# Row variances: other rows per partition, 64 KiB per partition and load, a quarter of each row on ScalarE

## Chip, cores, metric

One core of a Trainium2 chip. The metric is the device time of one execution in microseconds (us); lower is better. A profile's span is about 1.8 us shorter than the measured time of the same execution. A packet is one record of a DMA engine's work, here one contiguous piece, one partition's share of a load. A load has landed, or is ready, when the last of the sixteen DMA engines has reported its share.

## The reference

```python
x: float32 (8192, 8192)
return np.var(x, axis=1)          # 8192 float32
```

The input is 268.4 MB. It has to be read once, and nothing else of any size is moved.

## The kernel before

A tile is 128 adjacent rows, one per partition, 32 KiB each. It is loaded by two DMAs of half a row, one on SyncE's queue and one on ScalarE's, into one of four buffers. VectorE does all sums: sixteen `bn_stats` (count, mean and sum of squares of a group of 512 elements) and one `bn_aggr` (which combines the groups) per row.

```python
FMAX = nc.vector.BN_STATS_FMAX                     # 512
x_t = x.rearrange("(t p) (s f) -> t p s f", p=P, f=FMAX)
out_t = out.rearrange("(t p) -> t p", p=P)
data = ctx.enter_context(tc.tile_pool(name="data", bufs=4))
...
def issue_dma(t):
    xt = data.tile([P, nsub, FMAX], mybir.dt.float32)
    for c in range(CH):                            # CH = 2
        dma_eng[c % 2].dma_start(out=xt[:, lo:hi, :], in_=x_t[t, :, lo:hi, :])

def compute(t):
    for j in range(nsub):                          # nsub = 16
        nc.vector.bn_stats(out=st[:, j, :], in_=xt[:, j, :])
    nc.vector.bn_aggr(out=mv, in_=st)
    nc.gpsimd.tensor_copy(out=var_all[:, t : t + 1], in_=mv[:, 1:2])
... # load tile t, compute tile t - 3
nc.tensor.transpose(vp, var_all, ident)            # [128, 64] -> [64, 128]
nc.scalar.copy(vs, vp)
nc.sync.dma_start(out=out_t, in_=vs)
```

Of the kernel before, what the change touches and what calls it, by code (L numbers as in the profile page):

```python
# [1 line left out]

# [5 lines left out]


@with_exitstack  # L10
def kernel(
    ctx: ExitStack,
    tc: tile.TileContext,
    x: bass.AP,
    out: bass.AP,
):
    nc = tc.nc
    P = 128
    n, m = x.shape

    FMAX = nc.vector.BN_STATS_FMAX
    assert m % FMAX == 0
    nsub = m // FMAX

    assert n % P == 0
    ntiles = n // P

    x_t = x.rearrange("(t p) (s f) -> t p s f", p=P, f=FMAX)
    out_t = out.rearrange("(t p) -> t p", p=P)

    data = ctx.enter_context(tc.tile_pool(name="data", bufs=4))
    stats = ctx.enter_context(tc.tile_pool(name="stats", bufs=8))
    singles = ctx.enter_context(tc.tile_pool(name="singles", bufs=1))
    psum = ctx.enter_context(tc.tile_pool(name="psum", bufs=1, space=bass.MemoryType.PSUM))
    outp = ctx.enter_context(tc.tile_pool(name="outp", bufs=1))

    var_all = singles.tile([P, ntiles], mybir.dt.float32)
    ident = singles.tile([P, P], mybir.dt.float32)
    make_identity(nc, ident)

    dma_eng = [nc.sync, nc.scalar]

    CH = 2
    spc = nsub // CH

    xts = [None] * ntiles
    LOOK = 3

    def issue_dma(t):
        xt = data.tile([P, nsub, FMAX], mybir.dt.float32)  # L50
        for c in range(CH):
            lo = c * spc
            hi = lo + spc
            dma_eng[c % 2].dma_start(out=xt[:, lo:hi, :], in_=x_t[t, :, lo:hi, :])  # L54
        xts[t] = xt

    def compute(t):
        xt = xts[t]
        st = stats.tile([P, nsub, nc.vector.BN_STATS_DIM], mybir.dt.float32)
        for j in range(nsub):  # L60
            nc.vector.bn_stats(out=st[:, j, :], in_=xt[:, j, :])  # L61
        mv = stats.tile([P, nc.vector.BN_AGGR_DIM], mybir.dt.float32)
        nc.vector.bn_aggr(out=mv, in_=st)  # L63
        nc.gpsimd.tensor_copy(out=var_all[:, t : t + 1], in_=mv[:, 1:2])  # L64

    for t in range(ntiles):
        issue_dma(t)
        if t >= LOOK:
            compute(t - LOOK)
    for t in range(ntiles - LOOK, ntiles):  # L70
        compute(t)

    vp = psum.tile([ntiles, P], mybir.dt.float32)
    nc.tensor.transpose(vp, var_all, ident)  # L74
    vs = outp.tile([ntiles, P], mybir.dt.float32)
    nc.scalar.copy(vs, vp)  # L76
    nc.sync.dma_start(out=out_t, in_=vs)


# [1 line left out]
_INS = ['x']  # L81
_OUTS = [((8192,), 'float32')]


# [23 lines left out]
```

## Time and profile before

655.47 us, median of 2 runs (655.24 to 655.69).

| | before |
|---|---|
| VectorE busy | 636.2 of 653.6 us |
| VectorE, one tile | 9.93 us |
| DMA, one tile (4.19 MB at 428 GB/s) | 9.80 us |
| last tile landed, first fifteen engines / sixteenth | 630.7 / 638.5 us |

Lines of the page of the kernel before: span; busy time, share and instruction count of each engine; busy tenths and GB/s in 40 equal slices; the chain that ended last by engine; the costliest group (busy us, mean ns of one, idle time before and what ended it).

```profile
span 653.6 us, 1512 instructions
...
PE 0.4 (0%) x1; PEld 0.1 (0%) x1; DVE 636.2 (97%) x1088; ACT 1.5 (0%) x2; POOL 12.4 (2%) x70
...
DVE  2999999999999999999999999999999999999997
...
DMA  8999999999999999999999999999999999999950
GB/s 369 433 430 425 427 432 428 425 431 428 427 428 430 427 427 430 427 427 428 428 426 431 427 429 427 426 429 428 428 427 430 427 428 429 429 425 430 429 222 2
...
DVE 88%; DMA 6%; issue 5%; SPq 0%; PE 0%; ACT 0%; POOLq 0%; POOL 0%
...
L61 DVE BATCH_NORM_STATS2 st<-xt 128x6 f32<-128x512 f32 x1024 | 610.1, 673 | 13.6 <-DMA xt<-in_x_dram 13.6
```

VectorE is busy 97% of the span and leads the chain with 88%; its `bn_stats` waited only 13.6 us for data, nearly all of it for the first tile. The DMA is full too, in all but the last two slices. The windows of the same kernel (length, busy us and instruction count of each engine, granted clock, DMA share, GB/s):

```profile
core 0: us, PE busy (x) PEld busy (x) DVE busy (x) ACT busy (x) POOL busy (x), PEclk, DMA share, GB/s
0.00:20.00 20.00, 0.00 (x0) 0.00 (x0) 7.14 (x13) 0.00 (x0) 0.70 (x6) 1.00 0.91 380
20.00:40.00 20.00, 0.00 (x0) 0.00 (x0) 19.79 (x35) 0.00 (x0) 0.37 (x2) 1.00 1.01 431
...
100.00:600.00 500.00, 0.00 (x0) 0.00 (x0) 500.00 (x856) 0.00 (x0) 9.16 (x50) 1.00 1.01 428
```

Here is the margin: the DMA moves 428 GB/s at a busy share of 1.0, which is 9.80 us per tile; VectorE uses 422 GB/s, 9.93 us per tile. VectorE is the bound by 1.3%. The end, in the chain in order of time (start, length, what):

```profile
630.40 8.91 DVE st L61 x16
...
639.77 0.58 DVE mv L63
...
650.18 0.43 PE vp L74
```

VectorE starts the last tile at 640.3 us, and the last share of that tile had landed at 638.5.

### The profile page before, as it was taken

How to read it: one execution, taken by the hardware profiler on the slowest of the kernel's cores; microseconds unless marked ns; L12 is line 12 of the kernel's file. 1: busy time of each engine (PE TensorE's matmuls, PEld its weight loads, DVE VectorE, ACT ScalarE, POOL GpSimd, SP SyncE). 2: the span in 40 equal slices, each digit the busy share in tenths (PEclk: the TensorE clock that was granted, in tenths of full speed). 3: DMA queues.
4: the chain of work that ended last, by engine and by line, in shares of the span. 5: the costliest groups of instructions: out<-in, count | busy, mean ns of one | idle time of the engine just before them, and what ended most of it. 6: DMA issues, size and time to landing. Idle time of an engine off the chain costs nothing.

```text
span 653.6 us, 1512 instructions
## 1 busy us (share of the span) xinstructions
PE 0.4 (0%) x1; PEld 0.1 (0%) x1; DVE 636.2 (97%) x1088; ACT 1.5 (0%) x2; POOL 12.4 (2%) x70
## 2 busy tenths in 40 slices
PE   0000000000000000000000000000000000000000
PEld 0000000000000000000000000000000000000000
DVE  2999999999999999999999999999999999999997
ACT  0000000000000000000000000000000000000000
POOL 0000000000000000000000000000000000000000
DMA  8999999999999999999999999999999999999950
GB/s 369 433 430 425 427 432 428 425 431 428 427 428 430 427 427 430 427 427 428 428 426 431 427 429 427 426 429 428 428 427 430 427 428 429 429 425 430 429 222 2
DMA packets 18524, 268.57 MB, mean 411 GB/s; under 512 B 2064, under 2 KB 2128, under 8 KB 2128
## 3 DMA queue, kind: packets, MB, share of 16 engines
q1 hardware_dynamic: 9296, 134.25, 48.4%
q10 hardware_dynamic: 9216, 134.22, 48.2%
q14 instruction: 12, 0.10, 0.0%
HBM read 268.44 MB, written 0.03 MB: 411 GB/s over the span
## 4 chain that ended last, share of the span: by engine, by line
DVE 88%; DMA 6%; issue 5%; SPq 0%; PE 0%; ACT 0%; POOLq 0%; POOL 0%
DVE st L61 82%; DMA xt<-in_x_dram 6%; DVE mv L63 5%; SPq L54 0%; PE vp L74 0%; ACT vs L76 0%; POOLq L103 0%; POOL var_all L64 0%
## 5 line engine op out<-in xcount | busy, mean ns | idle before, releaser
L61 DVE BATCH_NORM_STATS2 st<-xt 128x6 f32<-128x512 f32 x1024 | 610.1, 673 | 13.6 <-DMA xt<-in_x_dram 13.6
L63 DVE BATCH_NORM_AGGREGATE mv<-st 128x2 f32<-128x96 f32 x64 | 36.4, 570 | 0.1
L64 POOL COPY var_all<-mv 128x1 f32<-128x1 f32 x64 | 11.7, 183 | 637.1 <-DVE mv L63 637.1
L76 ACT ACT_TABLE_LOAD x1 | 1.3, 1283 | 609.9 <-DMA xt<-in_x_dram 609.9
L74 PE MATMUL vp<-ident,var_all 128*64 128x128 f32 x1 | 0.4, 421 | 650.2 <-POOL var_all L64 650.2
L76 ACT COPY vs<-vp 64x128 f32<-64x128 f32 x1 | 0.3, 258 | 39.5 <-PE vp L74 39.5
masks.py:199 POOL TENSOR_SCALAR_AFFINE_SELECT ident<-ident 128x128 f32<-128x128 f32 x1 | 0.3, 292 | 0.1
L74 PEld LDWEIGHTS vp<-ident,var_all 128*64 128x64 f32 x1 | 0.1, 128 | 650.2 <-POOL var_all L64 650.2
masks.py:197 POOL MEMSET ident<- 128x128 f32 x1 | 0.2, 204 | 0.3 <-POOLq L92 0.3
L92 POOL MEMSET const-float32-0.0<- 128x1 f32 x1 | 0.1, 98 | 0.2 <-issue 0.2
L92 POOL MEMSET const-bfloat16-1.0<- 128x1 bf16 x1 | 0.1, 101 | 0.0
L92 POOL MEMSET const-uint8-127<- 128x1 uint8 x1 | 0.1, 101 | 0.0
L92 POOL MEMSET const-float32-1.0<- 128x1 f32 x1 | 0.1, 98 | 0.0
## 6 DMA issues: line engine op xcount, KB each, us to landing
xt<-in_x_dram ACTq DMA_DIRECT2D x64, 2048.0 KB, 29.1
xt<-in_x_dram SPq DMA_DIRECT2D x64, 2048.0 KB, 28.9
out_dram<-vs SPq DMA_DIRECT2D x1, 32.0 KB, 1.8
```

Of the source, the lines that this page charges most:

```text
L61: nc.vector.bn_stats(out=st[:, j, :], in_=xt[:, j, :])
L63: nc.vector.bn_aggr(out=mv, in_=st)
L64: nc.gpsimd.tensor_copy(out=var_all[:, t : t + 1], in_=mv[:, 1:2])
L74: nc.tensor.transpose(vp, var_all, ident)
L76: nc.scalar.copy(vs, vp)
L92: nc = _bacc.Bacc("TRN2", target_bir_lowering=False, num_devices=1)
```

## The change

Its intent: take a quarter of the sums from VectorE, use long contiguous reads, drop the transposition of the output. Each partition owns 64 adjacent rows. One load is two rows of each partition (64 KiB contiguous, 8 MiB in all), on one queue, into one of three buffers. ScalarE sums the last quarter of each row in two passes (sum and sum of squares about the mean of the first group), GpSimd turns that into the form that `bn_aggr` takes. The last row comes in shrinking pieces, so that little is left to do when the last one lands.

```diff
-    x_t = x.rearrange("(t p) (s f) -> t p s f", p=P, f=FMAX)
-    out_t = out.rearrange("(t p) -> t p", p=P)
-    data = ctx.enter_context(tc.tile_pool(name="data", bufs=4))
+    x_t = x.rearrange("(p t j) f -> t p (j f)", p=P, j=J)          # J = 2
+    out_p = out.rearrange("(p r) -> p r", p=P)
+    data = ctx.enter_context(tc.tile_pool(name="data", bufs=3))
...
+    def row_stats(xt, j):
+        for c in range(DC):                                        # 12 groups of 512
+            bn(st, c, xt[:, o + c * F : o + (c + 1) * F])
+        k = st[:, 1:2]
+        src = xt[:, o + DC * F : o + m]                            # 2048 elements
+        nc.scalar.activation(out=junk, in_=src, func=ACTF.Identity, bias=k, scale=-1.0,
+                             accum_out=s12[:, 0:1])
+        nc.scalar.activation(out=junk, in_=src, func=ACTF.Square, bias=k, scale=-1.0,
+                             accum_out=s12[:, 1:2])
+        ... # five small GpSimd operations put (count, mean, sum of squares) into st
...
+    for t in range(NT - 1):                                        # NT = 32
+        xt = data.tile([P, J * m], FP32, name="xt")
+        nc.sync.dma_start(out=xt, in_=x_t[t])
+        ... # row_stats of both rows, bn_aggr one row later
+    nc.sync.dma_start(out=xt[:, 0:m], in_=x_t[t, :, 0:m])          # last load: row 62
+    pieces = [4096, 2048, 1024, 512, 256, 256]                     # row 63, all on VectorE
...
-    nc.tensor.transpose(vp, var_all, ident)
-    nc.scalar.copy(vs, vp)
-    nc.sync.dma_start(out=out_t, in_=vs)
+    nc.sync.dma_start(out=out_p, in_=var_all[:].rearrange("p t j -> p (t j)"))
```

The 128 pieces of one load used to start 32 KiB apart in HBM. Now they start 64 rows apart, which is 2 MiB.

More of the change, by code (lines that the diff above doesn't have):

```diff
@@ L5 @@
 from concourse import bass_utils, mybir
-from concourse.masks import make_identity
 from concourse._compat import with_exitstack
+FP32 = mybir.dt.float32
+ACTF = mybir.ActivationFunctionType
+ALU = mybir.AluOpType
 @with_exitstack
@@ L19 @@
     n, m = x.shape
-    FMAX = nc.vector.BN_STATS_FMAX
-    assert m % FMAX == 0
-    nsub = m // FMAX
-    assert n % P == 0
-    ntiles = n // P
-    x_t = x.rearrange("(t p) (s f) -> t p s f", p=P, f=FMAX)
-    out_t = out.rearrange("(t p) -> t p", p=P)
-    data = ctx.enter_context(tc.tile_pool(name="data", bufs=4))
-    stats = ctx.enter_context(tc.tile_pool(name="stats", bufs=8))
+    F = nc.vector.BN_STATS_FMAX
+    J = 2
+    NT = n // (P * J)
+    C = m // F
+    AC = 4
+    DC = C - AC
@@ L33 @@
+    NA = AC * F
+    T3 = 3
+    x_t = x.rearrange("(p t j) f -> t p (j f)", p=P, j=J)
+    out_p = out.rearrange("(p r) -> p r", p=P)
+    data = ctx.enter_context(tc.tile_pool(name="data", bufs=3))
+    stats = ctx.enter_context(tc.tile_pool(name="stats", bufs=6))
+    small = ctx.enter_context(tc.tile_pool(name="small", bufs=6))
     singles = ctx.enter_context(tc.tile_pool(name="singles", bufs=1))
     psum = ctx.enter_context(tc.tile_pool(name="psum", bufs=1, space=bass.MemoryType.PSUM))
-    outp = ctx.enter_context(tc.tile_pool(name="outp", bufs=1))
@@ L37 @@
-    var_all = singles.tile([P, ntiles], mybir.dt.float32)
-    ident = singles.tile([P, P], mybir.dt.float32)
-    make_identity(nc, ident)
-    dma_eng = [nc.sync, nc.scalar]
-    CH = 2
-    spc = nsub // CH
-    xts = [None] * ntiles
-    LOOK = 3
-    def issue_dma(t):
-        xt = data.tile([P, nsub, FMAX], mybir.dt.float32)
-        for c in range(CH):
-            lo = c * spc
-            hi = lo + spc
-            dma_eng[c % 2].dma_start(out=xt[:, lo:hi, :], in_=x_t[t, :, lo:hi, :])
-        xts[t] = xt
@@ L57, in compute @@
-    def compute(t):
-        xt = xts[t]
-        st = stats.tile([P, nsub, nc.vector.BN_STATS_DIM], mybir.dt.float32)
-        for j in range(nsub):
-            nc.vector.bn_stats(out=st[:, j, :], in_=xt[:, j, :])
-        mv = stats.tile([P, nc.vector.BN_AGGR_DIM], mybir.dt.float32)
-        nc.vector.bn_aggr(out=mv, in_=st)
-        nc.gpsimd.tensor_copy(out=var_all[:, t : t + 1], in_=mv[:, 1:2])
-    for t in range(ntiles):
-        issue_dma(t)
-        if t >= LOOK:
-            compute(t - LOOK)
@@ L70, with bn @@
-    for t in range(ntiles - LOOK, ntiles):
-        compute(t)
-    vp = psum.tile([ntiles, P], mybir.dt.float32)
-    nc.tensor.transpose(vp, var_all, ident)
-    vs = outp.tile([ntiles, P], mybir.dt.float32)
-    nc.scalar.copy(vs, vp)
-    nc.sync.dma_start(out=out_t, in_=vs)
+    var_all = singles.tile([P, NT, J], FP32)
+    junk = psum.tile([P, NA], FP32)
+    def bn(st, at, src):
+        nc.vector.bn_stats(out=st[:, at * 6 : at * 6 + 6], in_=src)
+    def row_stats(xt, j):
+        st = stats.tile([P, DC * 6 + T3], FP32)
+        s12 = small.tile([P, 2], FP32)
+        tmp = small.tile([P, 2], FP32)
+        o = j * m
+        for c in range(DC):
[6 more added lines that the diff above has]
+                             accum_out=s12[:, 1:2])
+        b = DC * 6
+        nc.gpsimd.memset(st[:, b : b + 1], float(NA))
+        nc.gpsimd.tensor_scalar(out=tmp[:, 0:1], in0=s12[:, 0:1], scalar1=1.0 / NA, scalar2=0.0,
+                                op0=ALU.mult, op1=ALU.add)
+        nc.gpsimd.tensor_tensor(out=st[:, b + 1 : b + 2], in0=k, in1=tmp[:, 0:1], op=ALU.subtract)
+        nc.gpsimd.tensor_tensor(out=tmp[:, 1:2], in0=s12[:, 0:1], in1=tmp[:, 0:1], op=ALU.mult)
+        nc.gpsimd.tensor_tensor(out=st[:, b + 2 : b + 3], in0=s12[:, 1:2], in1=tmp[:, 1:2], op=ALU.subtract)
+        return st
@@ new lines, in finish @@
+    def finish(st, t, j):
+        mv = small.tile([P, 2], FP32)
+        nc.vector.bn_aggr(out=mv, in_=st)
+        nc.gpsimd.tensor_copy(out=var_all[:, t, j : j + 1], in_=mv[:, 1:2])
+    pending = []
+    for t in range(NT - 1):
+        xt = data.tile([P, J * m], FP32, name="xt")
+        nc.sync.dma_start(out=xt, in_=x_t[t])
+        for j in range(J):
+            st = row_stats(xt, j)
+            pending.append((st, t, j))
+            if len(pending) > 1:
+                finish(*pending.pop(0))
@@ new lines @@
+    t = NT - 1
+    xt = data.tile([P, J * m], FP32, name="xt")
+    nc.sync.dma_start(out=xt[:, 0:m], in_=x_t[t, :, 0:m])
+    pieces = [4096, 2048, 1024, 512, 256, 256]
+    lo = m
+    for w in pieces:
+        nc.sync.dma_start(out=xt[:, lo : lo + w], in_=x_t[t, :, lo : lo + w])
+        lo += w
+    st = row_stats(xt, 0)
+    finish(*pending.pop(0))
+    stl = stats.tile([P, (C + 1) * 6], FP32, name="stl")
+    lo, i = m, 0
+    while lo < 2 * m:
+        w = F
+        if 2 * m - lo <= 512:
+            w = 256
+        bn(stl, i, xt[:, lo : lo + w])
+        lo += w
+        i += 1
+        if i == 2:
+            mv = small.tile([P, 2], FP32)
+            nc.vector.bn_aggr(out=mv, in_=st)
+            nc.gpsimd.tensor_copy(out=var_all[:, t, 0:1], in_=mv[:, 1:2])
@@ L81 @@
+    mv = small.tile([P, 2], FP32)
+    nc.vector.bn_aggr(out=mv, in_=stl[:, 0 : i * 6])
+    nc.vector.tensor_copy(out=var_all[:, t, 1:2], in_=mv[:, 1:2])
+    nc.sync.dma_start(out=out_p, in_=var_all[:].rearrange("p t j -> p (t j)"))
 _INS = ['x']
```

## The prediction

> **What bounds the kernel now.** VectorE. The page gives it 636.2 us of a 653.6 us span; the chain of waits is 88% VectorE, and its timeline has no idle time after the fourth tile: one tile (16 bn_stats, 1 bn_aggr) every 9.93 us. The DMA is close behind: busy share 1.0 and 428 GB/s in every window from 60 to 600 us, about 9.8 us a tile. So removing VectorE work uncovers the DMA at once. The landing records add: fifteen of the sixteen engines deliver the last tile by 630.7 us, the sixteenth at 638.5. The instruction queue's 8 KiB fetches (twelve after the start) seem to fall on that one; each adds 0.65 to 1 us of lag. VectorE starts the last tile at 640.3 us: even now 2 us of slack.
>
> **What the change does.**
> - VectorE: 773 instead of 1024 bn_stats (cadence 0.59 us), shorter bn_aggr (0.49 us now, about 0.43): 7.5 us a row, 15 us per two-row load. Busy falls to about 490 us.
> - ScalarE: 126 activations of 2048 elements. The Trainium skill, "ScalarE: Activation LUTs", section "What ACT_TABLE_LOAD costs", gives about 1.99 us each with a pointer bias; this trace has none to compare. About 8 us per load, off the path. GpSimd: six small operations a row (0.1 to 0.2 us each), off the path.
> - DMA: same bytes, one queue, 64 KiB per packet instead of 16 KiB. In the packet records a 16 KiB packet takes 611 to 615 ns, a 4 B one 9 ns; if 9 ns is the fixed cost, a 64 KiB packet takes about 2415 ns. Estimate: 19.33 us per 8 MiB load, 434 GB/s, against 19.6 us for two tiles now.
>
> **The critical path after.** DMA until the last full load has landed, then VectorE. Start 1.8 us, 31 loads x 19.33 = 599.1, 1.2 us to land, about 6.5 us lag of the fetching engine: landed at about 608.6 us. From there VectorE works through two rows (15.0 us), row 0 of the last load (7.5) and all 17 pieces of the last row (10.7): about 33.3 us, while the DMA ends after 19 to 20. So the shrinking last pieces buy nothing: their data lie ready. Store and end 2.8 us. Span about 644.7 us; the measured time is 1.9 us above the span of before, so 646.5 us. Of the 140 us that VectorE loses, 9 reach the time.
>
> **Predicted:** 646.5 us, 80% range 640 to 660. Faster by over 2% (under 642.4): 0.15. Within 2%: 0.70. Slower: 0.15.
>
> **What the profile would show.** VectorE near 490 us, about 4 us idle before each load, released by the DMA; 432 to 434 GB/s in the middle; packets of 64 KiB near 2.4 us; one engine landing 5 to 8 us after the others; VectorE without idle for the last 33 us, the DMA quiet for the last 14; ScalarE about 250 us.
>
> **What would make it wrong.**
> - The rows of one load are now 2 MiB apart in HBM. The Trainium skill, "DMA: Bandwidth & Descriptors", section "Latency and other measured facts", has copies of 16 KiB pieces at that pitch at 164 instead of 207 GB/s per direction; no run here shows it yet. If it holds here, the time passes 780 us. I expect the longer pieces to hide most of it.
> - No fixed cost per packet: 428 GB/s stays, 653 us.
> - Packets cut to 32 KiB: 2 us more.
> - No lag of one engine: 640 us, just over 2% faster.
> - A bubble between loads on the single queue: each 0.1 us costs 3 us.

## The result, and the profile after

654.5 us, median of 2 runs (654.23 to 654.78); ratio to the kernel before 0.9986, 95% interval 0.9967 to 1.0005. It is the same within 2%. (A ratio is the mean time of one kernel's runs over that of the other's of the same rounds, so it is not quite the ratio of the medians.) The range held the time, and "within 2%" was the likeliest of the three classes. That says little: the class spans 642.4 to 668.6 us. A gain of 9 us was forecast, and 1 us was measured.

The same lines of the page of the changed kernel:

```profile
span 653.0 us, 1896 instructions
...
DVE 485.3 (74%) x838; ACT 265.2 (41%) x253; POOL 59.0 (9%) x382
...
DVE  0359677788777779777779777679777679776798
...
DMA  9999999999999999999999999999999999999970
GB/s 333 365 397 401 426 434 426 434 442 434 418 434 446 438 418 439 442 438 413 442 438 434 418 442 442 430 422 438 442 434 418 442 442 430 422 434 442 406 257 5
...
DMA 72%; DVE 26%; issue 1%; SPq 0%; DVEq 0%
...
L47 DVE BATCH_NORM_STATS2 st<-xt 128x6 f32<-128x512 f32 x756 | 451.6, 677 | 164.9 <-DMA xt<-in_x_dram 164.9
L60 ACT ACTIVATE junk<-xt,st 128x2048 f32<-128x2048 f32 x63 | 124.2, 1971 | 342.5 <-DVE st L47 342.5
...
L62 ACT ACTIVATION_READ_ACCUMULATOR junk<-xt,st 128x1 f32 x63 | 11.8, 187 | 0.0
```

VectorE fell from 636 to 485 us, as forecast (490), and its `bn_stats` now wait 164.9 us for the DMA instead of 13.6. ScalarE's activations take 1.97 us each. The chain is now 72% DMA. Look at the row of GB/s: 333, 365, 397, 401, and only then 426 and more. The kernel before was at 433 in its second slice. The windows of the changed kernel:

```profile
core 0: us, DVE busy (x) ACT busy (x) POOL busy (x), PEclk, DMA share, GB/s
0.00:20.00 20.00, 0.00 (x0) 0.00 (x0) 0.34 (x6) 1.00 0.96 344
20.00:40.00 20.00, 12.67 (x22) 9.66 (x9) 1.46 (x9) 1.00 0.99 374
40.00:60.00 20.00, 13.30 (x24) 7.13 (x7) 1.67 (x11) 1.00 0.98 396
60.00:80.00 20.00, 13.54 (x24) 6.87 (x7) 1.34 (x9) 1.00 0.99 417
...
100.00:600.00 500.00, 384.71 (x665) 213.28 (x205) 47.76 (x307) 1.00 1.00 433
```

From 100 to 600 us it runs at 433 GB/s, the forecast rate, faster than the 428 before. In the first 60 us it runs at 344, 374 and 396. The chain at the end, in order of time:

```profile
572.79 44.53 DMA xt<-in_x_dram
...
617.41 7.29 DVE st L47 x13
...
639.52 1.22 DVE stl L47 x2
...
641.13 8.33 DVE stl L47 x15
...
649.48 0.63 DVE mv L114
...
650.13 0.15 DVE var_all L115
```

The last full load is waited for until 617.4 us. From there on VectorE works without a pause for 32.9 us (forecast 33.3), the store adds 2.7 (forecast 2.8). So the tail is right, and all of the miss lies before 617.4 us, where 608.6 was forecast.

The packet records place it. A 64 KiB packet takes 2.42 us in the steady state (median; forecast 2.415). In the first 5 us the mean is 3.54 us, from 0 to 50 us it is 2.77 us with 75% of the packets over 2.46; after 75 us almost all are at 2.42. The first five loads were ready at 27.3, 49.1, 70.6, 90.5 and 110.0 us: the steps of 21.8, 21.5, 19.9 and 19.5 us approach the forecast 19.3.

### The profile page after: what moved, and what is told of

Read it like the earlier page. It is cut to its first block, busy times and chain, and to the rows that moved or that the text cites. A ratio compares the mean times of both kernels' runs of the same rounds, so it can differ in the third digit from the quotient of the medians.

```text
span 653.0 us, 1896 instructions
## 1 busy us (share of the span) xinstructions
DVE 485.3 (74%) x838; ACT 265.2 (41%) x253; POOL 59.0 (9%) x382
## 4 chain that ended last, share of the span: by engine, by line
DMA 72%; DVE 26%; issue 1%; SPq 0%; DVEq 0%
DMA xt<-in_x_dram 72%; DVE st L47 24%; DVE stl L47 1%; DVE mv L114 0%; DVE mv L75 0%; DVE mv L111 0%; SPq L81 0%; DVEq L47 0%; DVE var_all L115 0%
## 5 line engine op out<-in xcount | busy, mean ns | idle before, releaser
L47 DVE BATCH_NORM_STATS2 st<-xt 128x6 f32<-128x512 f32 x756 | 451.6, 677 | 164.9 <-DMA xt<-in_x_dram 164.9
L60 ACT ACTIVATE junk<-xt,st 128x2048 f32<-128x2048 f32 x63 | 124.2, 1971 | 342.5 <-DVE st L47 342.5
L62 ACT ACTIVATE junk<-xt,st 128x2048 f32<-128x2048 f32 x63 | 124.2, 1972 | 2.0
L66 POOL TENSOR_SCALAR tmp<-s 128x1 f32<-128x1 f32 x63 | 12.1, 192 | 397.3 <-ACT junk L60 397.3
L75 DVE BATCH_NORM_AGGREGATE mv<-st 128x2 f32<-128x75 f32 x62 | 25.8, 456 | 0.0
L70 POOL TENSOR_TENSOR st<-s,tmp 128x1 f32<-128x1 f32 x63 | 12.1, 191 | 99.0 <-ACT junk L62 99.0
L68 POOL TENSOR_TENSOR st<-st,tmp 128x1 f32<-128x1 f32 x63 | 12.1, 192 | 5.2
L69 POOL TENSOR_TENSOR tmp<-s,tmp 128x1 f32<-128x1 f32 x63 | 12.1, 191 | 0.0
L62 ACT ACTIVATION_READ_ACCUMULATOR junk<-xt,st 128x1 f32 x63 | 11.8, 187 | 0.0
L60 ACT ACTIVATION_READ_ACCUMULATOR junk<-xt,st 128x1 f32 x63 | 11.7, 186 | 0.0
L47 DVE BATCH_NORM_STATS2 stl<-xt 128x6 f32<-128x512 f32 (+1 forms) x17 | 9.6, 638 | 0.0
L65 POOL MEMSET st<- 128x1 f32 x63 | 6.2, 99 | 0.3 <-POOLq L131 0.3
L111 DVE BATCH_NORM_AGGREGATE mv<-st 128x2 f32<-128x75 f32 x1 | 0.5, 474 | 0.0
```

Source lines behind the costliest of these rows:

```text
L47: nc.vector.bn_stats(out=st[:, at * 6 : at * 6 + 6], in_=src)
L60: nc.scalar.activation(out=junk, in_=src, func=ACTF.Identity, bias=k, scale=-1.0, accum_out=s12[:, 0:1])
L62: nc.scalar.activation(out=junk, in_=src, func=ACTF.Square, bias=k, scale=-1.0, accum_out=s12[:, 1:2])
L65: nc.gpsimd.memset(st[:, b : b + 1], float(NA))
L66: nc.gpsimd.tensor_scalar(out=tmp[:, 0:1], in0=s12[:, 0:1], scalar1=1.0 / NA, scalar2=0.0, op0=ALU.mult, op1=ALU.add)
L68: nc.gpsimd.tensor_tensor(out=st[:, b + 1 : b + 2], in0=k, in1=tmp[:, 0:1], op=ALU.subtract)
```

## The experiments

Theory P: the 2 MiB pitch. Every load asks sixteen DMA engines to walk in step through pieces whose HBM addresses differ by multiples of 2 MiB; they collide there and slow each other, until the delays have driven them apart. Rival Q: a start-up cost of one queue with 64 KiB packets, whatever the addresses. Rival R: a cost of first touching 128 far-apart regions. A second question is the tail (theory T). Twelve kernels ran; e2, e3, e4, e5 and e13 once each (state unknown), the others with three rounds.

### e1_near_rows: the pitch alone, 64 KiB instead of 2 MiB

```diff
-    x_t = x.rearrange("(p t j) f -> t p (j f)", p=P, j=J)
+    x_t = x.rearrange("(t p j) f -> t p (j f)", p=P, j=J)
```

> The changed kernel with one line altered: one load takes 256 adjacent rows, so that the partitions' 64 KiB pieces lie 64 KiB apart in HBM instead of 2 MiB; packets, queue, buffers and arithmetic stay (the results come out in another row order, wrong on purpose). Theory P (the 2 MiB pitch makes the sixteen engines collide in HBM until they have drifted apart, and this costs the first 70 us about 10 us): the first load is ready at about 22 us instead of 27.3, packets take 2.42 us from the start, the last full load is ready at about 607 us instead of 617.3, time about 644.5 us (ratio to before 0.983). Rival Q (a start-up cost of one queue with 64 KiB packets, whatever the addresses): first load at 27 us, 617 us, time 654.5 us as the changed kernel (ratio 0.999).

647.08 us (644.5 expected), ratio 0.9876 (0.9859 to 0.9892), results in another order as intended. Its windows, in the same columns as those of the changed kernel:

```profile
0.00:20.00 20.00, 0.00 (x0) 0.00 (x0) 0.34 (x6) 1.00 1.00 419
20.00:40.00 20.00, 15.08 (x26) 9.66 (x9) 1.85 (x12) 1.00 0.97 419
40.00:60.00 20.00, 15.08 (x26) 8.38 (x8) 1.85 (x12) 1.00 0.97 419
...
100.00:600.00 500.00, 386.95 (x667) 215.56 (x206) 46.91 (x305) 1.00 1.00 433
```

The weak start is gone: 419 in the first window, which includes the 1.8 us before the first byte, against 344. Ready times of the loads (last of the sixteen engines, from the landing records, us):

```
load                     0      1      2      3      4      8     16      30
changed kernel       27.31  49.09  70.64  90.53 110.00 187.38 343.48  617.32
near rows            22.62  41.92  61.77  81.07 100.42 178.79 335.55  609.42
difference            4.69   7.17   8.87   9.46   9.58   8.59   7.93    7.90
```

The loss builds up over four loads, to 9.6 us, and no more comes after. The 609.4 us here are nearly what the forecast had assumed (608.6) for the changed kernel. Rival Q falls as the main cause: queue, packets and buffers are the same. A small part of the slow start remains with near rows: packets take 2.88 us in the mean of the first 5 us (3.54 with far rows). That the engines come apart can be read from the landings: those of the first load lie within 2.5 us of each other in the changed kernel, those of the fifth within 4.4 us, more than the 2.42 us of a packet. With near rows it is 0.6 and 0.9 us.

### e2_pitch_63_rows: nearly the same addresses, no power of two

```diff
+    x_63 = x[0 : 63 * P, :].rearrange("(p r) f -> p (r f)", p=P)
+    x_t = [x_63[:, min(J * t, 61) * m : (min(J * t, 61) + J) * m] for t in range(NT)]
```

> The changed kernel, but the partitions' pieces lie 63 rows (2 MiB less 32 KiB) apart instead of 64 rows; nearly the same addresses are touched by each load, spread over nearly the same 256 MiB, with the same packets and queue (results wrong on purpose). Theory P, in the form that it is the power of two that makes them collide: first load at about 22 us, last full load at about 607 us, time about 644.5 us. Rival R (the first touch of 128 far-apart regions costs, whatever their exact distance) and rival Q: first load at 27 us, time about 654.5 us.

647.10 us (one run), the last full load ready at 609.6 us. Its output is wrong, which doesn't matter for the time. The row of GB/s of its page, to set beside that of the changed kernel (333, 365, 397, 401):

```profile
GB/s 390 451 406 443 447 415 439 451 415 431 455 414 431 455 415 431 451 414 435 447 418 435 443 422 432 447 427 422 451 435 415 447 435 418 451 427 415 423 247 2
```

Pieces 1.97 MiB apart cost nothing against near rows; 2 MiB apart cost 8 us. So it is the pitch's exact size and not the distance: rival R falls. Only these three pitches were tried. 64 KiB is a power of two as well and does no harm, so the runs give no rule for other pitches.

### e3_before_far_rows: the pitch alone, in the kernel before

```diff
-    x_t = x.rearrange("(t p) (s f) -> t p s f", p=P, f=FMAX)
+    x_t = x.rearrange("(p t) (s f) -> t p s f", p=P, f=FMAX)
```

> The kernel before with one line altered: each partition owns 64 adjacent rows, so the rows of one tile lie 2 MiB apart; still 16 KiB packets, two queues and all sums on VectorE (row order of the result wrong on purpose). Theory P: packets of more than 611 ns at the start, decaying as the engines drift apart, some 10 us lost, time 660 to 670 us since VectorE is then starved at the start. If the figure of the Trainium skill for 16 KiB pieces holds throughout (164 of 207), about 340 GB/s and 790 us or more. Rival Q: nothing changes, 655.5 us.

662.12 us (one run), 6.7 us over the kernel before. So the pitch costs 16 KiB packets too. Here they do not come to rest so soon: the mean packet is 719 ns in the first 10 us (650 in the kernel before), and single stretches of 10 us reach 676 ns even at 350 us (the best is 611; the kernel before stays under 619 after its first 10 us). The lasting loss of a fifth that the Trainium skill's figure suggests for 16 KiB pieces ("DMA: Bandwidth & Descriptors", "Latency and other measured facts") was not seen: 407 GB/s over the span against 411. The page's figure is for copies between HBM tensors, these are loads only; the measurement decides.

### e4_far_rows_one_buffer and e5_near_rows_one_buffer: all engines start every load together

```diff
-    data = ctx.enter_context(tc.tile_pool(name="data", bufs=3))
+    data = ctx.enter_context(tc.tile_pool(name="data", bufs=1))
```

e5 has the line of e1 besides.

> The changed kernel with one data buffer instead of three: each load is issued only when the load before has been used up, so that all engines start each load together, from rest. Theory P: every load takes as long as the first of the changed kernel, about 26.5 us from issue to landing, with packets of 2.4 to 3.9 us to the end of the run. Rivals R and Q's form of a once-only cost (a cold start): only the first load takes 26.5 us, the later ones about 20.5 to 21 us. Time about 1320 us under P, about 1140 us under R.

> The partner of the one-buffer run with far rows: the same single buffer, but the partitions' pieces lie 64 KiB apart (result in another order on purpose). Theory P: each load takes about 21 us from issue to landing instead of 25.7, packets of 2.42 us apart from the very first ones; time about 1284 less 31 x 4.7, so about 1140 us. If the long landing of the far rows comes from the single buffer or from starting at rest and not from the pitch, it stays at 25 to 26 us and the time near 1284 us.

1284.3 us and 1161.8 us (one run each). The DMA issues (KB each missing for mixed sizes; median us from issue to landing), far rows first, then near rows:

```profile
xt<-in_x_dram SPq DMA_DIRECT2D x31, 25.7
```

```profile
xt<-in_x_dram SPq DMA_DIRECT2D x31, 21.8
```

With far rows the median load takes 25.7 us (at most 26.8), like the first load of the changed kernel (26.6), to the end of the run: the mean packet is 2.82 us before 100 us and 2.85 us after 600 us. With near rows it is 21.8 us and 2.50 us throughout. So it is no cost of a cold start. It comes back each time the engines start together, and where loads are queued back to back it wears off. (My 21 us for the near rows was a little low: the first sixteen packets of each load are slow there too, 3.07 us in the mean; the others take 2.42. With far rows the first sixteen take 3.54 us and the later ones still 2.64 to 2.79.)

### e8_before_scalar_quarter: ScalarE's share alone

The kernel before with its layout, queues and store, twelve groups on VectorE and the last quarter on ScalarE:

```diff
-        for j in range(nsub):
-            nc.vector.bn_stats(out=st[:, j, :], in_=xt[:, j, :])
...
+        for j in range(DC):                        # 12
+            nc.vector.bn_stats(out=st[:, j * 6 : j * 6 + 6], in_=xt[:, j, :])
+        act_part(st, DC * 6, st[:, 1:2], xt[:, DC:nsub, :].rearrange("p s f -> p (s f)"), s12, tmp)
... # act_part: the two activations and five GpSimd operations of the change
```

> The kernel before, with its layout, two queues, 16 KiB packets and transposed store, but ScalarE sums a quarter of each row as in the change. The DMA keeps its pace (last tile landed by its slowest engine at about 638.5 us); VectorE then does twelve sums (7.1 us), the aggregate, transpose and store, about 11 us, span about 649.7, time about 651.5 us (ratio 0.994). So VectorE's 140 us give 4 us here, because the DMA stands right behind it; if VectorE's time counted in full, it would be near 510 us.

653.13 us, ratio 0.9966 (0.9951 to 0.9981). Busy times, chain by engine, and VectorE's largest group:

```profile
PE 0.4 (0%) x1; PEld 0.1 (0%) x1; DVE 484.3 (74%) x832; ACT 269.6 (41%) x258; POOL 58.3 (9%) x390
...
DMA 80%; DVE 18%; issue 2%; POOL 0%; SPq 0%; PE 0%; DVEq 0%; ACT 0%; POOLq 0%
...
L93 DVE BATCH_NORM_STATS2 st<-xt 128x6 f32<-128x512 f32 x768 | 464.1, 675 | 161.1 <-DMA xt<-in_x_dram 161.1
```

VectorE lost 152 us of work and the time 2.2 us. The rest turned into 161 us of waiting for the DMA, which leads the chain with 80%. The 1.6 us beyond my figure are at the end. The last tile had landed at 636.6 us, 1.9 us earlier than I assumed, but the rest took longer: three `bn_aggr` were left, and two of them waited 1.1 us each for GpSimd's small operations.

### e6_far_rows_fine_tail: the tail alone

Row 60 whole, rows 61 and 62 in halves, row 63 in nine pieces, and its first quarter to ScalarE:

```diff
-    pieces = [4096, 2048, 1024, 512, 256, 256]
+    for t, cuts in ((NT - 2, ([m], [m // 2, m // 2])),
+                    (NT - 1, ([m // 2, m // 2], [NA, 1024, 1024, 1024, 1024, 1024, 512, 256, 256]))):
...
+    act_part(stl, len(widths) * 6, k, src, *part)   # first quarter of row 63
```

> The changed kernel with the 2 MiB pitch kept, but the last two loads cut into pieces earlier (row 60 whole, rows 61 and 62 in halves, row 63 in nine pieces) and ScalarE given the first quarter of the last row too. Theory T (the 33 us after the last full load are VectorE work that waits for whole 8 MiB loads, not the DMA): VectorE keeps up with the landings, the DMA ends at about 639 us as now and the kernel about 4.8 us later, span about 643.7, time about 645.5 us, 9 us less than the changed kernel. If the tail is bound by the DMA, nothing is gained: 654 us.

651.59 us, ratio 0.9944 (0.9929 to 0.9959): 3 us gained, not 9. Windows near the end (columns as above):

```profile
610.00:620.00 10.00, 10.00 (x18) 6.46 (x8) 1.49 (x10) 1.00 1.00 418
620.00:630.00 10.00, 9.80 (x18) 4.19 (x4) 1.04 (x7) 1.00 1.02 308
630.00:640.00 10.00, 8.76 (x16) 6.51 (x7) 1.45 (x9) 1.00 0.81 213
```

The DMA falls to 308 and 213 GB/s while it still has data to move, and the last piece lands at 646.2 us instead of 639 (the profile is of the slowest of the four runs, 653.04 us). The small pieces start 2 MiB apart as well, and are slow again: 4 KiB packets take 250 ns in the mean here and 163 ns in the next run, which differs in the pitch. All packets of 1 to 32 KiB in the tail together cost 5.9 us more per engine than there. The tail was the right place, but with far rows this cut gained a third of what was expected. Why the small pieces are slow although the engines had come apart by then was not tested.

### e7_near_rows_fine_tail: both repairs

As e6, with the line of e1; two transposes on TensorE and a copy put the results in order.

> Both repairs together, with correct results: near rows (64 KiB pitch) and the fine tail; the order of the rows is put right at the end by two transposes on TensorE and one copy, about 1 us more. If the two losses add: the last piece lands at about 629 us, end about 634.9, time about 636.8 us, ratio to before 0.972. If the gains overlap, not below 643 us.

642.41 us, ratio 0.9805 (0.9789 to 0.9822), results correct; the interval does not settle whether it is faster by 2%. VectorE near the end, in order of time:

```profile
590.46 14.34 DVE L50 BATCH_NORM_STATS2 st<-xt 128x6 f32<-128x512 f32 x24 [5.25 <-DMA xt<-in_x_dram]
...
620.96 7.16 DVE L50 BATCH_NORM_STATS2 st<-xt 128x6 f32<-128x512 f32 x12
628.21 0.49 DVE L78 BATCH_NORM_AGGREGATE mv<-st 128x2 f32<-128x75 f32 x1
628.62 7.21 DVE L50 BATCH_NORM_STATS2 stl<-xt 128x6 f32<-128x512 f32 x13
```

The DMA was done at 629.7 us as expected, but VectorE started the last row at 628.6, when nearly all of it lay ready. It had waited for the last whole load until 590.4 us, and from then on had a backlog: it gains only 2.2 us per row (9.7 for the DMA, 7.5 for VectorE), and five rows were too few. So my estimate of 636.8 had let it catch up too early.

### e10_near_rows_finer_tail: ten rows to catch up in

Against e7:

```diff
-    for t in range(NT - 2):
+    for t in range(NT - 5):                        # whole loads
...
+    half = [m // 2, m // 2]
+    for t, cuts in ((NT - 5, ([m], [m])), (NT - 4, ([m], [m])), (NT - 3, ([m], half)),
+                    (NT - 2, (half, half)), (NT - 1, ...as e7...)):
```

> As the run with both repairs, which gave 642.4 us and not the expected 636.8, since VectorE was still one backlog of about 5 us behind from the last whole load and never caught up (it gains only 2.2 us on the DMA per row). Here the last five loads come in rows or half rows, so that it has ten rows to catch up in. If that reading is right: DMA ends at about 630.2 us, the kernel 5.8 us later, time about 637.9 us, ratio 0.973. If instead the DMA's small pieces cost what is gained, 641 to 643 us.

638.49 us, ratio 0.9743 (0.9727 to 0.9759), results correct. It beats the kernel before by 2.6% and the changed kernel by 2.4% (the latter from the medians, of different rounds). VectorE at the end:

```profile
624.85 0.49 DVE L78 BATCH_NORM_AGGREGATE mv<-st 128x2 f32<-128x75 f32 x1 [2.19 <-POOL st L62]
625.26 7.21 DVE L50 BATCH_NORM_STATS2 stl<-xt 128x6 f32<-128x512 f32 x13
632.58 0.52 DVE L126 BATCH_NORM_AGGREGATE mv<-stl 128x2 f32<-128x81 f32 x1
```

The last row is begun at 625.3 us, its last piece lands at 630.1 and VectorE is done with it 3.2 us later. On its way there VectorE waited again: three `bn_aggr` near the end stood 6.2 us in all until GpSimd had finished with ScalarE's quarter of the row (the first line above shows one of these waits). No run tried whether the time falls without them.

### e11, e12, e13: standing apart on purpose

If the collisions end because the engines drift apart, setting them apart at the start should spare the loss with the pitch unchanged. e11 queues seven small DMAs for 14, 12, ... 2 partitions on ScalarE's queue before the loads, whose data nobody uses:

```diff
+    for c in range(7):
+        i, p0, lo = 14 - 2 * c, c // 4 * 64, c % 4 * 4096
+        nc.scalar.dma_start(out=dm[p0 : p0 + i, lo : lo + 4096], in_=x[16 * c : 16 * c + i, 0:4096])
```

> The changed kernel with the 2 MiB pitch kept (correct results); before the loads seven small DMAs of 16 KiB pieces for 14, 12, 10, ... 2 partitions, whose data nobody uses, are queued, so that the engines enter the first load at eight different times, up to 4.3 us apart; they add about 0.9 MB. Theory P in its full form (the collisions come from the engines walking in step and end when they are apart): packets reach 2.42 us within the first load or two, the last full load is ready at 611 to 614 us instead of 617.3, time 648 to 651 us although more bytes are moved. If standing apart does not help, the collisions last their 70 us again and the extra bytes make it 655 us or more.

666.49 us, ratio 1.0162. It told nothing: the small packets stood behind 64 KiB packets of the other queue, took up to 2.5 us each and were not all done until 52.6 us (the next expectation says 55). e12 puts them first on the queue of the loads, from few to many partitions; e13 is the same with near rows.

```diff
+    for c in range(7):
+        i, p0, lo = 2 + 2 * c, c // 2 * 32, c % 2 * 8192
+        nc.sync.dma_start(out=dm[p0 : p0 + i, lo : lo + 6144], in_=x[16 * c : 16 * c + i, 0:6144])
```

> A better form of the stagger: in the run before, the small DMAs sat on a second queue, each of their packets stood behind a 64 KiB packet of the load, and they were not done until 55 us; so it told nothing. Here seven small DMAs (24 KiB pieces for 2, 4, ... 14 partitions) go first on the queue of the loads[...]. The 2 MiB pitch is kept, results are correct. Theory P in full (in step they collide, apart they do not): the gap in the landing of the last full load to the partner run with near rows, which is 7.9 us without stagger (617.3 against 609.4), shrinks to under 3 us; last full load at about 614 to 616, time about 652. If standing apart does not help, the gap stays near 8 us and the last full load is at about 621, time 658.

> The partner: the same seven small DMAs first, with the 64 KiB pitch (row order of the result wrong on purpose). It shows what the small DMAs themselves cost where there is nothing to mend: the last full load at about 609.4 plus 4 us, 613.5, time about 651.

669.75 us and 669.93 us. The price of the small DMAs was far off: they cost 23 us with near rows, not 4. The Trainium skill, "SBUF — State Buffer", section "Door 1: The DMA port swizzle", may bear on it: it has partitions 0 to 15 on four of the sixteen ports, at 104 GB/s. The small DMAs go to at most 14 adjacent partitions each, and the trace has 110 to 128 GB/s in the first 20 us and 3.6 us for many a 24 KiB packet. But the 64 KiB packets beside them were slow too (up to 11.1 us), and no run sends the small DMAs to other partitions, so this cause is not shown. The comparison for which the pair was run does not depend on it: VectorE waits for the last full load until 632.4 us with far rows and 632.7 us with near rows, here one after the other:

```profile
632.40 14.34 DVE L47 BATCH_NORM_STATS2 st<-xt 128x6 f32<-128x512 f32 x24 [4.27 <-DMA xt<-in_x_dram]
```

```profile
632.73 14.34 DVE L47 BATCH_NORM_STATS2 st<-xt 128x6 f32<-128x512 f32 x24 [4.27 <-DMA xt<-in_x_dram]
```

The gap of 7.9 us is gone. Windows of e12, with far rows:

```profile
30.00:40.00 10.00, 0.00 (x0) 0.00 (x0) 0.00 (x0) 1.00 0.97 419
40.00:60.00 20.00, 13.07 (x22) 9.66 (x9) 1.46 (x9) 1.00 1.01 436
```

The first load is still under way at 30 us, and from there the 2 MiB pitch runs at full rate (packets of 2.42 us in the mean), where the changed kernel needed 75 us for that. So engines that enter the loads apart do not collide with 64 KiB packets, even at this pitch. One caution: the small DMAs let the engines into the first load over some 20 us (its packets begin at 5.5 us, the last small one ends at 26.4), so the pair does not show how little would do.

## Why the prediction was right and wrong

- **The DMA stands right behind VectorE, so little of VectorE's gain reaches the time.** Right. Alone, the ScalarE share took 152 us from VectorE and gave 2.2 us (e8).
- **A fixed cost of 9 ns per packet, so 64 KiB packets run at 434 GB/s.** Right: 2.42 us per packet, 433 GB/s in the windows, 19.35 us per load in the steady state. The loads of near rows were ready at 609.4 us against 608.6 forecast.
- **VectorE's 33 us at the end, with the shrinking pieces for nothing.** Right: 32.9 us; the last piece lay ready at 638.9 us and VectorE came to the last row at 639.5.
- **"I expect the longer pieces to hide most of it."** This is the step that failed. The prediction named the 2 MiB pitch as the chief danger, thought of it as all or (nearly) nothing, lasting or absent, and put 0 us into its sum. The runs showed a third thing: a loss at the start that wears off, 9.6 us by the fifth load and 7.9 us at the last full load (e1 against the changed kernel). That is small against the 130 us and more that a lasting loss would have cost by the prediction's own figure, so "most" was hidden; but the whole forecast gain was 9 us, and a term of 8 us that is left out decides it. With the pitch alone altered the changed kernel takes 647.08 us, 0.6 us from the 646.5 forecast.
- **The lag of the engine that fetches instructions, about 6.5 us.** The size held, its source only in part. Without the lag the forecast had the last full load at 602.1 us; in e1 the first engine landed its share of it at 602.6 us and the last one 6.9 us later. But only 4.0 us of that lie between the last two engines (in the changed kernel too); two others had fallen behind as well, by 2.2 and 2.9 us.
- **ScalarE off the path.** Right; it is busy 265 us and not 250, since each summing activation is followed by a further instruction of 187 ns.

What stays open: where in HBM the engines collide. The runs show that for 64 KiB packets 2 MiB does it and one row less does not (e2), that it comes back with each common start (e4 against e5), and that it is gone when the engines enter apart (e12 against e13). For shorter packets standing apart is not the whole story: 16 KiB packets had slow stretches at 350 us (e3), and the small pieces at the end were slow although the engines were apart (e6). No run looks into HBM, so banks or channels are only a guess.

## What to carry to other kernels

When an engine is 97% busy, compare its time per tile with the DMA's: the gap between the two, here 1.3%, is all that less work on that engine can win before the DMA is the bound. When a change gives each partition its own block of rows, look at the distance between the partitions' addresses; at exactly 2 MiB the loads ran 18, 11 and 5% below the rate of near rows in the first three windows of 20 us, and small pieces at the end were slow again; one row less, or adjacent rows per load, mended the loads. A tail is cut only if the working engine has caught up before it begins: cut the loads finer several rows ahead, not only the last.

## What the Trainium skill lacked or had wrong

- "DMA: Bandwidth & Descriptors", "Latency and other measured facts", on the pitch of HBM rows: it gives one lasting rate per pitch (164 of 207 GB/s at 2 MiB), for copies between HBM tensors in 16 KiB pieces, which no run here repeats. Loads in 16 KiB pieces kept 407 of 411 GB/s. For loads of 64 KiB pieces the loss was confined to the first 75 us (344, 374, 396 GB/s, and 433 from 100 us on), came back at each common start (25.7 against 21.8 us per load) and was gone when the engines entered apart. A pitch smaller by one row of 32 KiB mended it fully (647.1 us).
- The same page does not give the time of one packet by its length for these queues: 16 KiB packets took 611 to 615 ns (428 GB/s), 64 KiB packets 2418 ns (433 GB/s).
- The same page names a runtime-internal queue beside the kernel's, but no page says what instruction fetches cost the loads. In the kernel before, the lag of one engine grew by about 1 us after nine of the twelve 8 KiB fetches, to 7.8 us at the end.
- "ScalarE: Activation LUTs", "What ACT_TABLE_LOAD costs": its 1.99 us for 2048 elements agrees (1.97 us), but an activation that also sums needs a further instruction of 187 ns, which the page does not have.
